# Moving splits, epilogues and scratch homes in a single-core fp32 encoder block

## The chip, the cores and the metric

One core of one Trainium2 chip runs the kernel. The metric is the device time of one execution in microseconds (us); lower is better. The engines are TensorE (PE, matmul; PEld is its weight load), VectorE (DVE), ScalarE (ACT), GpSimd (POOL) and SyncE (SP); each runs its own queue of instructions in the order in which the program issues them.

## The reference, cut to what matters

One residual block of an encoder over 256 tokens with 2048 channels, all in float32:

```python
h = x + 0.5 * swiglu(rms_norm(x, ffn1_norm), ...)      # hidden width 5632
u = rms_norm(h, mix_norm)
z_pool, q, k, v = split(u @ w_in)                      # 1024 columns each
y_pool = pool_mixer(z_pool, pool_w, pool_scale)        # 4 groups, windows 2/4/8/16
y_attn = chunk_attention(q, k, v, ...)                 # 8 heads of 128
g_pool, g_attn = split(sigmoid(u @ w_branch_gate + b_branch_gate))
h = h + (g_pool * (y_pool @ w_br_pool) + g_attn * (y_attn @ w_br_attn)) @ w_out
h = h + 0.5 * swiglu(rms_norm(h, ffn2_norm), ...)
h = h + sigmoid(rms_norm(h, ple_norm) @ w_ple_gate) * (p @ w_ple)
```

`swiglu(x, g, u, d)` is `(silu(x @ g) * (x @ u)) @ d`. Every `rms_norm` divides a token's row by its root mean square and multiplies by a gain per channel.

## The kernel before

**Matmuls in three passes.** TensorE multiplies in the float32r type, and full accuracy comes from splitting each operand into a high part (a cast) and a low part (the rest). A weight tile `wraw` of 4 x 128 rows by 512 columns is loaded by DMA; ScalarE casts it to `whi` (line 163) and VectorE subtracts to get `wlo` (line 171). `high_passes` (lines 206, 208) multiplies `whi` by the low and the high part of the activations, `low_passes` (line 213) multiplies `wlo` by the high part: twelve matmuls of 512 columns per weight tile and token tile. There are two token tiles (t = 0, 1) of 128 tokens. Two `wlo` and three `whi` buffers exist.

**Items and the stream.** An `Item` is one weight tile's work. `stream` walks a flat list and in round i issues `high` of item i+2, `low` of item i+1 and then the matmuls of item i, so the order of instructions on PE, DVE and ACT is the order written here. Loads are issued up to five items ahead, in list order, while a room for the tile is free. `seven` is an item with one token tile's worth of matmuls (twelve), `both` one with two (twenty-four).

**Blocks.** `block` computes a 1024-column output pair from the first two blocks of 512 rows with seven products instead of eight (items p1 to p7, on sums of weights made in place at lines 439, 443 and 446, called t1, t2 and t4, and on sums of activations held by `Pair`), and from the remaining rows with `both` items h[0] to h[3]. The accumulators are named a, b (second half of the columns) and e, d (first half). A feed-forward layer's hidden width is cut into parts of 4, 4 and 3 blocks of 512; in each part come the up/gate blocks and then two `down` blocks over that part. The `down` blocks of the last part of 3 have one remaining row block (`nr` = 1); all others have two. With `nr` = 2 the last item h[3] is carried over and runs as second item of the next block.

**Deferred work.** `later(n, task)` puts a task off by n steps; each `seven` takes one step and each `both` takes a step before each token tile, and a step issues the tasks that are due. If an item's operand is not there yet, it takes further steps at once (`while o.missing: step()`). `split` issues the ACT cast of an activation tile at once and its DVE subtraction one step later.

**Norms.** `Norm.turn` transposes a 128 x 512 piece of h on PE (line 506) into one of two PSUM buffers with tag `tp`, multiplies by the gain and hands the result to a `Pair` (column blocks b = 0, 1) or an `Operand` (b = 2, 3). The norms with a `home` (the first, the third and the last) build sums in `Pair.take`: for b = 1 the gained tile `gained` is, after the first norm, a `brief_tile`, which is one of the same two `tp` PSUM buffers, and so is the difference `s3` (row name `s`). `piece_tile` is a ring of five SBUF tiles.

**Mixer.** Between the projections' items the heads run as tasks: `scores`, `exps`, `shares`, `keys_down`, `values`; the four pooling groups as `means`, `read`, `group_map`. All use the two `tp` buffers.

**Launch.** `load_x` issues six dummy matmuls on the identity, loads the first norm's gain and x, turns block 0 and queues the other blocks' turns.

Of the kernel before, what the change touches and what calls it, by code (L numbers as in the profile page):

```python
# [10 lines left out]
F32 = mybir.dt.float32  # L11
# [30 lines left out]
def hybrid_block(ctx: ExitStack, tc: tile.TileContext, a: dict, out: bass.AP):  # L42
# [72 lines left out]
    def split(hi, lo, src, then):  # L115
# [119 lines left out]
    def both(banks, operand, then=None, last=False, first=False):  # L235

        def mm(it):
# [5 lines left out]
            for t, acc in enumerate(accs):  # L243
# [5 lines left out]
                low_passes(acc, forms, it.lo, last)  # L249
            if then:  # L250
                then(accs)
# [73 lines left out]
    class Pair:  # L325
# [6 lines left out]
        def __init__(self, pool, tag, home=None, other=None):  # L332
            self.pool, self.tag, self.home = pool, tag, home
# [17 lines left out]
        def take(self, half, b, t, src):  # L351
            def sums():
# [5 lines left out]
                if (b, t) == (0, 1):  # L358
                    s3 = brief_tile("s3")
# [40 lines left out]
    def block(sides, pair, rest, nr, k0, taken, done2, done1, alone=False):  # L400
# [48 lines left out]
        def rest_item(i, side, last, then=None):  # L449
# [4 lines left out]
                both(lambda: [acc(n)() for n in names], lambda: rest()[i], then, last),  # L454
            )

        end2 = lambda accs: done2(*accs)
        end1 = lambda accs: done1(*accs)
# [13 lines left out]
        if nr == 2:  # L472
            h = [rest_item(0, 1, False), rest_item(1, 1, True, end2),
                 rest_item(0, 0, False), rest_item(1, 0, True, end1)]
            return begin + [h[0], p6, p2, p7, h[1], p4, h[2]], [h[3]]
        h = [rest_item(0, 1, True), rest_item(0, 0, True)]
        p7.mm = seven(acc("b"), form("S3"),
                      lambda: (taken("u3", bank["b"]), done2(bank["e"], bank["d"])))
        p4.mm = seven(acc("b"), form("A22"), lambda: done1(bank["a"], bank["b"]), True)
        return begin + [h[0], p6, p2, p7, h[1], p4], []  # L480
# [38 lines left out]
    class Norm:  # L519
# [21 lines left out]
        def turn(self, b, t, early=False):  # L541
# [4 lines left out]
            if early or (self.home and b < 2):  # L546
                f = u.place(t) if b == 0 else (piece_tile if early else brief_tile)("gained")
# [49 lines left out]
    def load_x(norm, first_weights):  # L597
# [13 lines left out]
        for b in range(D // NB):  # L611
            norm.open(b)
            for t in token_tiles(b):
# [3 lines left out]
                else:  # L617
                    later(3 * b, task)
        for b in range(D // NB):
# [7 lines left out]
    class Parts:  # L627
# [3 lines left out]
        def __init__(self, tile_=piece_tile):  # L631
            self.tile = tile_
# [32 lines left out]
    def ffn(norm, following, gate, up, down, flat, carry, begins=False, before=None, after=None):  # L665
# [8 lines left out]
        for part, nblk in enumerate(FFN_PARTS):  # L674
# [20 lines left out]
            for j in range(nblk):  # L695
# [21 lines left out]
                else:  # L717
                    parts = Parts()

                    def done2(e, d, parts=parts):  # L720
                        parts.sg = []
                        for t, s in ((0, parts.c12(e)), (1, parts.c22(d))):
                            nc.scalar.activation(s, s, AF.Silu, scale=norm.r[t])
                            parts.sg.append(s)

                    def done1(a_, b_, j=j, parts=parts, state=state):
                        s0, s1 = parts.sg
                        h0 = parts.c11(a_)
                        nc.vector.scalar_tensor_tensor(
                            s1, b_, norm.r[1], s1, op0=ALU.mult, op1=ALU.mult  # L730
                        )
                        nc.vector.scalar_tensor_tensor(
                            h0, h0, norm.r[0], s0, op0=ALU.mult, op1=ALU.mult
                        )
                        take(j, [h0, s1], state)
# [11 lines left out]
            for n in range(0, D // NB, 2):  # L747
# [16 lines left out]
                def done2(e, d, n=n, last=last):  # L764
                    add(0, n, e)
                    add(1, n, d)
                    if last:
                        following.take(n)

                def done1(a_, b_, n=n, last=last):  # L770
                    add(0, n + 1, a_)
                    add(1, n + 1, b_)
                    if last:
# [493 lines left out]
```

## Time and profile before

| what | value |
|---|---|
| device time, median of 3 (range) | 2124.25 us (2123.97 to 2124.56) |
| device time of the profiled execution | 2124.25 us |
| its span, first to last instruction | 2122.1 us |
| PE busy | 2064.5 us, 97% of the span, 9206 matmuls |
| DVE busy | 1669.0 us, 79% |
| ACT busy | 1143.6 us, 54% |
| POOL busy | 66.0 us, 3% |
| mean granted TensorE clock | 0.991 |
| DMA | 444 MB, 209 GB/s over the span |

The busy time is the union of an engine's instructions. The device time of the profiled execution equals the median, and 2.15 us of it lie outside the span. The sites of the change are short against the whole, so stretches of a few microseconds have to be read one by one.

### The profile page before, as it was taken

The numbers are of one execution on the slowest core, as the hardware profiler recorded it, in microseconds if no ns is written. First come the engines' busy times: TensorE is split into PE (matmuls) and PEld (weight loads), VectorE is DVE, ScalarE is ACT, GpSimd is POOL, SyncE is SP. The second block draws the span as 40 slices with busy tenths as digits, with TensorE's granted clock in tenths as the row PEclk, the third lists the DMA queues.
The fourth block names the chain that finished last, engine by engine and source line by source line (L and its number), as shares of the span: only waits on it lengthen the run. The fifth ranks groups of instructions, "written<-read, shape, count | busy, mean of one in ns | idle before, by whom it ended". The sixth has DMA issues, their size and how long they took to land.

```text
span 2122.1 us, 22846 instructions
## 1 busy us (share of the span) xinstructions
PE 2064.5 (97%) x9206; PEld 1691.9 (80%) x9206; DVE 1669.0 (79%) x1259; ACT 1143.6 (54%) x988; POOL 66.0 (3%) x89
## 2 busy tenths in 40 slices
PE   7999999999999999999999999999999999999898
PEld 6888888888887788887888887888888888887677
DVE  5898888898898966554555557898888898898987
ACT  5665556555665644453434455665556655564663
POOL 0000000000000000000000000000000000000000
PEclk9999999999999999999999999999999999999999
DMA  7675677577756655554656555776577667755664
GB/s 259 217 220 196 229 257 228 179 239 253 222 180 209 217 188 192 182 169 144 204 191 198 198 183 181 258 239 215 193 264 236 198 203 265 231 193 162 224 194 159
DMA packets 222442, 444.02 MB, mean 209 GB/s; under 512 B 7480, under 2 KB 7552, under 8 KB 222336
## 3 DMA queue, kind: packets, MB, share of 16 engines
q1 hardware_dynamic: 201968, 400.59, 54.0%
q0 software_dynamic: 20368, 41.98, 10.3%
q8 instruction: 72, 1.18, 0.2%
q14 instruction: 34, 0.28, 0.0%
HBM read 440.44 MB, written 2.10 MB: 209 GB/s over the span
## 4 chain that ended last, share of the span: by engine, by line
PE 81%; DVE 13%; issue 3%; DMA 2%; ACT 1%; POOL 0%; SPq 0%; DVEq 0%; ACTq 0%; POOLq 0%
PE acc L206 8%; PE acc L208 8%; PE acc L213 8%; DVE wlo L171 7%; PE accb L206 7%; PE accb L213 7%; PE accb L208 7%; PE acce L213 5%; PE accd L206 4%; PE accd L208 4%; PE accd L213 4%; PE acca L213 4%; PE acca L206 4%; PE acca L208 4%; DVE wraw L446 4%
## 5 line engine op out<-in xcount | busy, mean ns | idle before, releaser
L171 DVE TENSOR_TENSOR wlo<-wraw,whi 128x2048 fp32r<-128x2048 f32 (+1 forms) x486 | 1099.6, 2274 | 316.3 <-PE acc L213 113.4
L163 ACT CAST whi<-wraw 128x2048 fp32r<-128x2048 f32 (+1 forms) x486 | 922.6, 1902 | 663.6 <-PE acc L208 174.7
L206 PE MATMUL acc<-whi,ulo 128*128 128x512 f32 x288 | 113.8, 395 | 0.0
L208 PE MATMUL acc<-whi,uhi 128*128 128x512 f32 x288 | 112.3, 390 | 0.0
L206 PE MATMUL acc<-whi,ual 128*128 128x512 f32 x216 | 87.5, 405 | 8.7 <-DVE ual L119 8.7
L208 PE MATMUL acc<-whi,uah 128*128 128x512 f32 x216 | 85.3, 395 | 0.0
L439 DVE TENSOR_TENSOR wraw<-wraw 128x2048 f32<-128x2048 f32 x35 | 80.2, 2292 | 1.2
L443 DVE TENSOR_TENSOR wraw<-wraw 128x2048 f32<-128x2048 f32 x35 | 80.2, 2292 | 1.2
L446 DVE TENSOR_TENSOR wraw<-wraw 128x2048 f32<-128x2048 f32 x35 | 79.9, 2283 | 0.0
L213 PE MATMUL acc<-wlo,uhi 128*128 128x512 f32 x288 | 77.1, 389 | 0.0
L206 PE MATMUL acce<-whi,ulo 128*128 128x512 f32 x184 | 73.3, 398 | 0.0
L208 PE MATMUL acce<-whi,uhi 128*128 128x512 f32 x184 | 71.8, 390 | 0.0
L206 PE MATMUL accd<-whi,ulo 128*128 128x512 f32 x184 | 71.8, 390 | 0.0
L208 PE MATMUL accd<-whi,uhi 128*128 128x512 f32 x184 | 71.7, 390 | 0.0
L206 PE MATMUL accb<-whi,ual 128*128 128x512 f32 x184 | 71.7, 390 | 0.0
L206 PE MATMUL accb<-whi,usl 128*128 128x512 f32 x184 | 71.7, 390 | 0.0
L208 PE MATMUL accb<-whi,uah 128*128 128x512 f32 x184 | 71.6, 389 | 0.0
L208 PE MATMUL accb<-whi,ush 128*128 128x512 f32 x184 | 71.6, 389 | 0.0
L206 PE MATMUL acca<-whi,ulo 128*128 128x512 f32 x184 | 71.6, 389 | 0.0
L208 PE MATMUL acca<-whi,uhi 128*128 128x512 f32 x184 | 71.6, 389 | 0.0
L206 PE MATMUL accb<-whi,ulo 128*128 128x512 f32 x184 | 71.6, 389 | 0.0
L208 PE MATMUL accb<-whi,uhi 128*128 128x512 f32 x184 | 71.6, 389 | 0.0
(332 smaller groups left out, 4211.4 us busy)
## 6 DMA issues: line engine op xcount, KB each, us to landing
wraw<-in_ffn_w_up_dram SPq DMA_DIRECT2D x88, 1024.0 KB, 7.5
wraw<-in_ffn_w_down_dram SPq DMA_DIRECT2D x88, 1024.0 KB, 9.1
wraw<-in_ffn_w_gate_dram SPq DMA_DIRECT2D x87, 1024.0 KB, 8.9
wraw<-in_w_in_dram SPq DMA_DIRECT2D x32, 1024.0 KB, 5.4
wraw<-in_w_branch_gate_dram SPq DMA_DIRECT2D x32, 1024.0 KB, 5.4
wraw<-in_ffn_w_gate_dram POOLq DMA_DIRECT2D x21, 1024.0 KB, 11.8
wraw<-in_w_out_dram SPq DMA_DIRECT2D x16, 1024.0 KB, 5.0
wraw<-in_w_ple_gate_dram SPq DMA_DIRECT2D x16, 1024.0 KB, 7.6
```

Source lines behind the costliest of these rows:

```text
L163: nc.scalar.copy(out=self.hi[:, ks, :], in_=w.raw[:, ks, :])
L171: nc.vector.tensor_tensor(out=self.lo[:, ks, :], in0=w.raw[:, ks, :], in1=self.hi[:, ks, :].bitcast(F32), op=ALU.subtract,)
L206: nc.tensor.matmul(acc, xl, wh[:, k, :], start=start and k == 0, stop=False, skip_group_check=True)
L208: nc.tensor.matmul(acc, xh, wh[:, k, :], start=False, stop=False, skip_group_check=True)
L213: nc.tensor.matmul(acc, xh, wl[:, k, :], start=False, stop=last and k == len(forms) - 1, skip_group_check=True)
L439: tt(b11.raw, b11.raw, b12.raw, op=ALU.add)
L443: tt(b11.raw, b11.raw, b22.raw, op=ALU.add)
L446: tt(b21.raw, b21.raw, b11.raw, op=ALU.add)
```

## The change

- `split` gets `at_once`: the subtraction is issued right behind the cast. The heads' `values` use it, and `group_map` of the pooling does the same for its own low part.
- `both` gets `each`, called behind each token tile's matmuls; the epilogues `done2` and `done1` of the feed-forward and the final blocks now take one token tile at a time. In the last block the outputs' order becomes t = 0, then t = 1.
- `Pair` gets `brief`: in the norms the difference `s3` is a `piece_tile` in SBUF, and so is `gained`. Hidden blocks keep the PSUM tile.
- In blocks with `nr` = 1 the order h[0], p6, p2, p7, h[1], p4 becomes p2, p6, h[0], p7, h[1], p4.
- `load_x` takes one step after block 0's turns and then issues ten dummy matmuls into the first `tp` tile.

```diff
+    def split(hi, lo, src, then, at_once=False):
         nc.scalar.copy(out=hi, in_=src)
...
-        later(1, low)
+        if at_once:
+            low()
+        else:
+            later(1, low)
...
                 low_passes(acc, forms, it.lo, last)
+                if each:
+                    each(t, acc)
...
-                    s3 = brief_tile("s3")
+                    s3 = self.brief("s3")
...
-        return begin + [h[0], p6, p2, p7, h[1], p4], []
+        return begin + [p2, p6, h[0], p7, h[1], p4], []
...
-                    self.pair = Pair(act, "u", self.home, other)
+                    self.pair = Pair(act, "u", self.home, other, piece_tile)
...
-                f = u.place(t) if b == 0 else (piece_tile if early else brief_tile)("gained")
+                f = u.place(t) if b == 0 else piece_tile("gained")
...
+            if b == 0:
+                step()
+                for _ in range(10):
+                    nc.tensor.matmul(tp[:, :P], ident, ident, start=True, stop=True)
...
-                    def done1(a_, b_, j=j, parts=parts, state=state):
-                        s0, s1 = parts.sg
-                        h0 = parts.c11(a_)
...
+                    def done1(t, acc, j=j, parts=parts, state=state):
+                        s = parts.sg[t]
+                        if t:
+                            nc.vector.scalar_tensor_tensor(
+                                s, acc, norm.r[1], s, op0=ALU.mult, op1=ALU.mult
+                            )
+                            take(j, [parts.h0, s], state)
+                        else:
+                            parts.h0 = parts.c11(acc)
+                            nc.vector.scalar_tensor_tensor(
+                                parts.h0, parts.h0, norm.r[0], s, op0=ALU.mult, op1=ALU.mult
+                            )
...
-            split(o.hi[:, hh % KB, :], o.lo[:, hh % KB, :], op[:, :SEQ], o.there)
+            split(o.hi[:, hh % KB, :], o.lo[:, hh % KB, :], op[:, :SEQ], o.there, True)
...
-                def low(yp=yp, yl=yl, yh=yh, c=c, o=o):
...
-                later(1, low)
+                nc.vector.scalar_tensor_tensor(
+                    yl, yp[:, :SEQ], col("pool_scale", c), yh.bitcast(F32),
+                    op0=ALU.mult, op1=ALU.subtract,
+                )
+                o.there()
...
+            def done1(t, acc, n=n, parts=parts, sg=sg, early=early):
+                s = late_tile("sg") if t else parts.c11(acc)
+                nc.scalar.activation(s, acc if t else s, AF.Sigmoid, scale=norm.r[t])
+                sg[1, t] = s
+                if early:
+                    embed(n + 1, t, early["accs"][t], s)
```

## Rows read from the trace of the kernel before

**Rows 1.** The page's busy times: us, share of the span, instructions.

```profile
PE 2064.5 (97%) x9206; PEld 1691.9 (80%) x9206; DVE 1669.0 (79%) x1259; ACT 1143.6 (54%) x988; POOL 66.0 (3%) x89
```

**Rows 2.** What TensorE waited for, whole span: us in total, times, longest.

```profile
PE acce L213 <- DVE wlo L171: 11.9, 15, 3.6
PE acc L206 <- DVE ual L119: 8.7, 1, 8.7
PE acce L206 <- DVE hidlo L119: 6.5, 2, 3.2
PE tp L506 <- DVE blocks L363: 5.2, 1, 5.2
PE tp L1002 <- DVE yattnlo L119: 2.7, 2, 2.0
...
PE tp L1002 <- ACT pt L948: 1.1, 1, 1.1
```

**Rows 3.** Timeline of the launch: start us, us, engine, line, operation, idle before.

```profile
6.67 1.51 DVE L549 TENSOR_TENSOR blocks<-tp,vcol 128x512 f32<-128x512 f32 x2 [0.87 <-PE tp L506]
...
8.21 0.62 ACT L116 CAST hidsh<-blocks 128x512 fp32r<-128x512 f32 x1 [0.20 <-DVE blocks L549]
8.74 1.99 ACT L163 CAST whi<-wraw 128x1024 fp32r<-128x1024 f32 x2
...
15.36 0.69 DVE L119 TENSOR_TENSOR ual<-blocks,uah 128x512 fp32r<-128x512 f32 x1
...
16.19 0.77 PE L206 MATMUL acc<-whi,ual 128*128 128x512 f32 x1 [8.74 <-DVE ual L119]
```

**Rows 4.** Busy time by stretch; PEclk is the granted TensorE clock.

```profile
16.20:24.10 7.90, 7.90 (x26) 6.35 (x27) 1.75 (x3) 1.40 (x2) 0.00 (x0) 0.70 0.82 304
...
1945.40:1952.60 7.20, 7.16 (x24) 5.75 (x25) 0.58 (x1) 0.67 (x1) 0.00 (x0) 0.76 0.00 0
...
1981.20:1992.20 11.00, 5.82 (x20) 4.85 (x21) 10.93 (x12) 8.40 (x13) 0.00 (x0) 0.69 0.27 50
```

**Rows 5.** Timeline, first block of the last part, second feed-forward.

```profile
1940.30 4.48 DVE L171 TENSOR_TENSOR wlo<-wraw,whi 128x2048 fp32r<-128x2048 f32 x2
...
1944.71 1.28 DVE L119 TENSOR_TENSOR hidlo<-tp,hidhi 128x512 fp32r<-128x512 f32 x2
...
1945.44 0.50 PE L206 MATMUL acce<-whi,hidlo 128*128 128x512 f32 x1 [3.23 <-DVE hidlo L119]
```

**Rows 6.** TensorE's timeline there: low passes of two token tiles in succession.

```profile
1966.49 1.07 PE L213 MATMUL accb<-wlo,hidhi 128*128 128x512 f32 x4
1969.21 1.07 PE L213 MATMUL accb<-wlo,hidah 128*128 128x512 f32 x4
```

**Rows 7.** Timeline, second block of that part (last norm's turns).

```profile
1982.76 2.29 DVE L171 TENSOR_TENSOR wlo<-wraw,whi 128x2048 fp32r<-128x2048 f32 x1
...
1986.38 1.09 PE L506 MATMUL tp<-ident,h 128*128 128x128 f32 x4 [5.22 <-DVE blocks L363]
...
1994.40 2.29 DVE L171 TENSOR_TENSOR wlo<-wraw,whi 128x2048 fp32r<-128x2048 f32 x1 [2.24 <-PE accd L213]
```

**Rows 8.** ScalarE's timeline there: gain multiplications into SBUF (blocks) and PSUM (gained).

```profile
1977.49 1.12 ACT L558 ACTIVATE blocks<-tp,vcol 128x128 f32<-128x128 f32 x4
...
1980.30 1.47 ACT L558 ACTIVATE gained<-tp,vcol 128x128 f32<-128x128 f32 x4
```

**Rows 9.** Timeline of the mixer, 956 to 966 us.

```profile
958.66 0.37 ACT L116 CAST yattnhi<-tp 128x256 fp32r<-128x256 f32 x1 [2.94 <-PE tp L956]
...
961.47 2.29 DVE L171 TENSOR_TENSOR wlo<-wraw,whi 128x2048 fp32r<-128x2048 f32 x1 [5.28 <-PE acc L213]
963.68 0.42 DVE L119 TENSOR_TENSOR yattnlo<-tp,yattnhi 128x256 fp32r<-128x256 f32 x1
```

**Rows 10.** Timeline of the end.

```profile
2115.84 0.69 DVE L1134 TENSOR_TENSOR sg<-acc,sg 128x512 f32<-128x512 f32 x1 [2.75 <-ACT sg L1151]
...
2117.28 1.66 SPq L1136 DMA_DIRECT2D out_dram<-h  x2
```

More of the change, by code (lines that the diff above doesn't have):

```diff
@@ L110, in step @@
             task()
-    def split(hi, lo, src, then):
+    def split(hi, lo, src, then, at_once=False):
         nc.scalar.copy(out=hi, in_=src)
@@ L233, in seven, with both @@
         return mm
-    def both(banks, operand, then=None, last=False, first=False):
+    def both(banks, operand, then=None, last=False, each=None):
         def mm(it):
@@ L325, in hybrid_block, with __init__ @@
     class Pair:
-        def __init__(self, pool, tag, home=None, other=None):
-            self.pool, self.tag, self.home = pool, tag, home
+        def __init__(self, pool, tag, home=None, other=None, brief=brief_tile):
+            self.pool, self.tag, self.home, self.brief = pool, tag, home, brief
             self.halves = [Half(self, b) for b in range(2)]
@@ L447, in t4, with rest_item @@
             b11.done()
-        def rest_item(i, side, last, then=None):
+        def rest_item(i, side, last, each=None):
             w, n0 = sides[side]
@@ L453, in rest_item, with ends @@
                 Weight(w, k0 + (2 + i) * KB, n0),
-                both(lambda: [acc(n)() for n in names], lambda: rest()[i], then, last),
+                both(lambda: [acc(n)() for n in names], lambda: rest()[i], None, last, each),
             )
-        end2 = lambda accs: done2(*accs)
-        end1 = lambda accs: done1(*accs)
+        def ends(done, names):
+            for t, n in enumerate(names):
+                done(t, bank[n])
         p1 = Item(b11, seven(acc("b"), form("A11"), tell("p1", "b")), [b11, b12], [t1], keep=True)
@@ L631, in __init__ @@
         def __init__(self, tile_=piece_tile):
-            self.tile = tile_
+            self.tile, self.sg = tile_, {}
         def taken(self, name, acc):
@@ L718, in ffn, with done2 @@
                     parts = Parts()
[L720 to L724, printed above, removed]
-                    def done1(a_, b_, j=j, parts=parts, state=state):
-                        s0, s1 = parts.sg
-                        h0 = parts.c11(a_)
[L729 to L735, printed above, removed]
+                    def done2(t, acc, parts=parts):
+                        s = (parts.c22 if t else parts.c12)(acc)
+                        nc.scalar.activation(s, s, AF.Silu, scale=norm.r[t])
+                        parts.sg[t] = s
+                    def done1(t, acc, j=j, parts=parts, state=state):
[10 more added lines that the diff above has]
+                            )
                     main, left = block(
@@ L762, in taken, with done2, done1 @@
                         add(1, n, acc, -0.5)
[L764 to L767, printed above, removed]
+                def done2(t, acc, n=n, last=last):
+                    add(t, n, acc)
+                    if last and t:
                         following.take(n)
[L770 to L773, printed above, removed]
+                def done1(t, acc, n=n, last=last):
+                    add(t, n + 1, acc)
+                    if last and t:
                         following.take(n + 1)
```

30 lines of the change are left out of this document (8 added, 22 removed).

## The prediction

> **What bounds the kernel now.** I read the page first: TensorE is busy 97% of the span [rows 1], so the most that any reordering can give back is TensorE's idle time, about 58 us, the end included. Then the waits of TensorE over the whole span [rows 2], to see who ends that idle time. The reader is to see that it isn't spread evenly. One group is a comb of waits for VectorE's `wlo` (11.9 us in 15), which the diff leaves alone in the blocks with `nr` = 2. The others are single holes: 8.7 us at the launch, twice 3.2 for `hidlo`, 5.2 for a `tp` buffer, a few in the mixer. Last I read the timeline around each hole, with the granted clock of the stretches, to see what the late instruction stands behind in its queue.
>
> One token tile's twelve matmuls take 2.72 us at the full clock: two successive low passes start at 1966.49 and 1969.21 [rows 6]. Call this a pass; a `seven` is one, a `both` two.
>
> **The change part by part.**
>
> *Launch.* The first product needs `ual`, which is issued one step after the cast, so behind both weight tiles' subtractions: it runs at 15.36, although `whi` started at 8.74 [rows 3]. TensorE idles 8.7 us, and then has the lower clock: in 16.2 to 24.1 the granted clock is 0.70 of full [rows 4], so 0.30 x 7.9 = 2.4 us are lost.
> With the added step VectorE does `ual`, `hidsl` and the difference s3 (0.6 to 0.7 us each) straight after its two gain multiplications, which end at 8.18: until 10.1. The cast of s3 (0.6) now stands in ScalarE's queue ahead of `whi`, whose first half comes at 11.7 instead of 9.7. The first product starts near 11.8: 4.4 us earlier. The ten dummies are fp32 of 128 columns; they follow the turns, whose eight matmuls end at 7.45. At the half clock a pair takes 0.5 us, as the first six took (12 instructions in about 2.9 us), at the full clock half of it, so the dummies end between 10.1 and 12.4. That is before or just after the product could start: they cost 0 to 0.6 and keep TensorE active in the hole. If the clock is full then, the whole 2.4 comes back less about 0.5 for the later `wlo`, and the gain is 6.3. If the engine falls to 1.2 GHz anyway for a few microseconds, it is 3.2 to 4.9. I take 5.8; bounds 3.2 to 6.6.
>
> *Blocks with `nr` = 1, first of each layer.* h[0] reads the third hidden block, whose transposes are issued two and three steps after the carried item. In the old order h[0] comes at once behind p3, takes further steps to get its operand, and its low parts stand behind two `wlo` (4.48 us from 1940.30) [rows 5]. With p2 and p6 ahead, the two low parts have two passes, 5.4 us, to be made in, and the hole was 3.2: it goes, in both layers. What moves with it: p2's load of `b21` goes ahead of h[0]'s in SP's list; its room is freed by the previous p4, some eight items earlier, and nothing waits behind it longer than now. t2, which p6 reads, has one item more ahead of it (p2) and lies two items back. p7 now follows a `both`, so t4 (2.29) is covered by two passes and the wait of 0.1 at h[1] goes too: 3.3 us per layer. In the second layer the clock after the hole was 0.76 over 7.2 us [rows 4], 1.7 us lost: 5.0 there. Bounds from zero clock effect to 1 us of small delays more: 3.2 to 4.4, and 3.4 to 6.0.
>
> *Second of these blocks, last norm.* TensorE waits 5.22 us for a `tp` buffer [rows 7]: `gained` sits in it until VectorE has subtracted and differenced it. In SBUF it holds no PSUM buffer, and this wait goes. But what is late next is VectorE: it is busy 10.93 of the 11.0 us around the hole [rows 4]. Before, five `wlo` had to be done for p1, p3, p5, h[0] and p6, which are six passes; in the new order p1, p3, p5, p2 and p6 need the same five `wlo` and are five passes. So for the same products TensorE needs one `wlo` (2.29) more from a VectorE that has no room. The gain is at most 5.2 - 2.3 = 2.9, or 2.2 if read as the 2.24 us that VectorE itself waited just after [rows 7] and now fills; at the low end new waits at p2 and p6 eat it all. I take 2.5; bounds 0 to 5.2. In the first layer the mixer's norm has no home, so its second block only gains the 0.1 at h[1] and a little order: 0.4, bounds -0.5 to 0.9.
> The four `gained` tiles also change their writer's target. Four pieces into PSUM take 1.47 us on ScalarE, into SBUF 1.12 [rows 8]: 0.35 less each, off the path where ScalarE has room, so nothing is counted.
> The Trainium skill, page "ScalarE: Activation LUTs", section "Step-by-step: what each stage is for", says the opposite: a ScalarE write to PSUM is faster than one to SBUF. By it these tiles would get dearer on ScalarE; by the row they get cheaper by 0.35. The trace does not agree with it for a group of four, and the sum is the same by either, since ScalarE has idle time around them.
>
> *Mixer.* The heads' low part leaves a `tp` buffer occupied until a step later, behind a `wlo`: the cast is done at 959.0, the subtraction runs at 963.68 behind the `wlo` from 961.47 [rows 9], and the pooling map waits 2.0 us for it; another 0.7 and, for the buffer of `pt`, 1.1 are of the same kind some 20 us before [rows 2]. At once, the subtraction runs near 959.1 and both buffers are free when the map comes: 2.7 + 1.1 = 3.8. VectorE now waits for ScalarE's cast in its queue; behind it stand the `wlo`, which themselves waited 5.28 us for a buffer [rows 9], so the wait is covered. Without that cover it would be the cast, 0.4, for each of 8 heads: 3 us. The pooling's low parts keep their place behind the same `wlo`, so the two waits around 985 us (a `tp` buffer, a DMA of pooling weights, 3.0 together) stay. 3.8; bounds 1.0 to 4.5.
>
> *Epilogues by token tile.* In the 31 blocks with `nr` = 2 the first tile's epilogue now stands ahead of the next step's tasks. At h[1] no task stands there, at h[3] VectorE may do its first two operations (0.7 each) during the second pass. No hole of [rows 2] lies behind them, so nothing, bounds -2 to 1.
>
> *End.* Of the last two output tiles the t = 1 one is now last and alone: its multiplication starts at 2115.84 and its DMA is issued at 2117.28 as now; the second tile's two operations and DMA, which end the old program (the pair of DMA issues lasts 1.66) [rows 10], go in front. 1.66 less one issue of 0.33: 1.3; bounds 0.8 to 1.5.
>
> **Sum.** 5.8 + 3.3 + 0.4 + 3.8 + 5.0 + 2.5 + 1.3 = 22.1 us. The profiled execution took 2124.25, equal to the median, so 2124.25 - 22.1 = 2102.2.
>
> **The rivals.**
> *VectorE takes over in the reordered blocks.* For it: 10.93 of 11.0 us [rows 4]. Against: it idles 2.24 us right after [rows 7]. Then the second blocks give nothing, and p2 or p6 waits also in the first ones: 2.5 + 0.4 + about 3 less, 2108.
> *The launch gains little.* s3's cast holds back `whi`, and the clock falls anyway, in the gap between dummies and product. For it: 8.7 us without matmuls is what it fell after. Against: the gap becomes 2 us at most. 3.2 or less instead of 5.8: 2105 to 2108.
> *It does not do what it should:* b21's load, moved ahead, is late, and p2 waits in the hole's place. A load takes some 5 to 9 us to land; the room comes free about 20 us before p2. If it does decide, 3.3 + 5.0 + 2.9 are lost: 2113.
> *Slower:* the early epilogue blocks VectorE. It is in order, so an epilogue that waits for the first pass holds the step's tasks, and behind them the next `wlo`, on which the comb of waits hangs. There are 62 such epilogues. At 0.36 us each it eats 22.1 and decides; at 0.5 the time is 2133. Against: before, two epilogues after the second pass stood ahead of the same `wlo`, and few tasks fall on those steps.
>
> **How the numbers follow.** The forecast with all five gains: 0.60. VectorE in the reordered blocks 0.14, little at the launch 0.14, the load 0.05, slower or nothing from the epilogues 0.07. The time is that of the first: 2102.2. All upper bounds together give about 2124.3 - 29, but not all meet: 2095 at the low end. At the high end the second and third cases give 2108, and lower bounds of two terms 2110. A difference under 0.2%, 4.25 us, can't be told from no change; faster means below 2120.0: all of the first four cases, 0.93. Within 0.2%: 0.04, slower 0.03, both from the epilogues' rival.
>
> **What would show it.** In the changed profile the first real product should start near 12 us, and the granted clock stay above 0.9 until 24. The waits for `hidlo`, `blocks` and `yattnlo` should be gone from TensorE's list, and the waits of p2 and p6 for `wlo` in the last part be new, some 1 to 2.5 us each. The wait of 3.6 for `wlo` at the last norm's reciprocal root stays, and so do those of the pooling weights. The last output DMA should be one, 1.3 us after the other's old place at most. I am wrong if VectorE's busy share rises without TensorE's, if `wlo` waits more than double, or if the blocks with `nr` = 2 get longer.

## The result

The changed kernel takes 2100.76 us (median of 4 runs, 2100.06 to 2101.72) beside 2124.4 us (4 runs, 2123.97 to 2126.38) for the kernel before: the ratio is 0.9887, 95% interval 0.987 to 0.9904. Its profiled execution took 2100.06 us with a span of 2098.0, so 24.1 us went out of the span.

The page's busy times of the changed kernel answer to [rows 1]. TensorE is 4.3 us less busy (it has twenty instructions more, and ran fewer stretches at the lower clock); VectorE has the same work in a shorter span.

```profile
PE 2060.2 (98%) x9226; PEld 1691.0 (81%) x9226; DVE 1669.5 (80%) x1259; ACT 1142.5 (54%) x988; POOL 66.0 (3%) x89
```

What TensorE waits for in the changed kernel, whole span, as in [rows 2]:

```profile
PE acce L216 <- DVE wlo L174: 12.2, 16, 3.6
PE accb L216 <- DVE wlo L174: 3.1, 2, 2.3
...
PE tp L1013 <- DMA gw<-in_pool_w_dram: 2.0, 1, 2.0
PE acca L216 <- DVE wlo L174: 2.0, 2, 1.6
...
PE acc L209 <- DVE ual L119: 1.1, 1, 1.1
PE tp L999 <- DVE ypoollo L1022: 1.1, 1, 1.1
PE acc L209 <- ACT whi L166: 0.8, 1, 0.8
...
PE tp L1013 <- ACT pt L959: 0.3, 1, 0.3
```

The big single holes of [rows 2] are gone: 8.7 us for `ual`, twice 3.2 for `hidlo`, 5.2 for `blocks`, 2.7 for `yattnlo`. New are 3.1 us of waits for `wlo` in the accumulator b, 1.1 for `ual` and 0.8 for `whi`; those for `wlo` in a have grown from 0.8 to 2.0. The comb on acce is as it was.

To see where the time went, I cut the span at the starts of matmuls that both traces have: the third weight tile's first, then p3 and the following p1 of each pair of `nr` = 1 blocks, the mixer's first projection and so on. The stretches are the differences of those starts, in us. "First" and "second" are the two `nr` = 1 blocks; the mixer's stretch is its heads and pooling; "end" runs from the last matmul's start.

| kernel | launch | first (ffn1) | second (ffn1) | mixer | first (ffn2) | second (ffn2) | last stage | end |
|---|---|---|---|---|---|---|---|---|
| before | 30.79 | 30.13 | 37.98 | 67.90 | 31.71 | 42.20 | 102.02 | 7.45 |
| changed | 26.03 | 25.94 | 36.72 | 63.89 | 25.94 | 39.81 | 101.60 | 6.11 |
| order only | 30.76 | 25.94 | 37.19 | 69.17 | 25.94 | 39.91 | 101.24 | 7.45 |
| homes only | 30.28 | 31.73 | 38.01 | 66.33 | 31.55 | 40.62 | 101.23 | 7.44 |
| no dummies | 26.23 | 25.94 | 37.17 | 65.50 | 25.94 | 39.87 | 101.84 | 6.09 |
| no step | 30.81 | 25.94 | 37.19 | 65.26 | 25.94 | 39.85 | 101.46 | 5.99 |
| old order in the second blocks | 26.15 | 25.94 | 37.82 | 65.07 | 25.94 | 40.89 | 101.39 | 6.02 |
| heads' split late | 26.12 | 25.94 | 37.15 | 68.36 | 25.94 | 39.82 | 101.80 | 5.98 |
| pooling's split late | 26.06 | 25.94 | 36.72 | 63.97 | 25.94 | 39.81 | 101.49 | 6.12 |
| epilogues behind both tiles | 26.11 | 25.94 | 37.16 | 65.02 | 25.94 | 39.87 | 101.46 | 5.99 |
| less VectorE | 26.04 | 25.94 | 34.40 | 62.21 | 25.94 | 37.65 | 99.06 | 6.03 |
| old order at the end | 26.00 | 25.94 | 36.67 | 62.21 | 25.94 | 39.81 | 102.35 | 7.45 |

The stretches left out (the rest of both feed-forwards and the projections) are the same to 0.3 us in all of these. The gains of the changed kernel are so 4.76 at the launch, 4.19 and 1.26 in ffn1, 4.01 in the mixer, 5.77 and 2.39 in ffn2, 0.42 in the last stage and 1.34 at the end, which is the whole 24.1 us. Two of them are in part the clock's: in ffn1's second block five other kernels with the same order have 37.15 to 37.19 us at a granted clock of 0.95, where the changed kernel has 1.00, so 0.8 of the 1.26 us are the change's; and the last stage takes 101.23 to 102.35 us in all the kernels but the one with less VectorE, whichever epilogues they have. The table also shows how far one execution's total can be trusted. Among kernels whose mixer waits alike, that stretch takes 62.2, 63.9 or 65.0 to 65.5 us: the granted clock over it is 1.00 at 62.21, 0.97 at 63.89 and 0.95 at 65.07. Totals differ by 3 us for that alone, so below an edit is judged by its own stretch. Where the clock is alike the mixer's gain is nearly the same: 66.33 against 62.21 us at 1.00, 67.90 against 63.89 at 0.97, and 69.17 against 65.0 to 65.5 at 0.95.

The launch of the changed kernel, as in [rows 3]:

```profile
7.65 3.75 PE L630 MATMUL tp<-ident 128*128 128x128 f32 x20
...
10.60 0.62 ACT L116 CAST ush<-s 128x512 fp32r<-128x512 f32 x1 [1.36 <-DVE s L365]
11.12 5.61 ACT L166 CAST whi<-wraw 128x1024 fp32r<-128x1024 f32 x4
...
12.21 0.50 PE L209 MATMUL acc<-whi,ual 128*128 128x512 f32 x1 [0.81 <-ACT whi L166]
...
14.58 0.38 SPq L147 DMA_DIRECT2D wraw<-in_ffn_w_up_dram  x1
...
20.89 1.91 ACT L166 CAST whi<-wraw 128x2048 fp32r<-128x2048 f32 x1 [4.16 <-DMA wraw<-in_ffn_w_up_dram]
...
26.03 0.50 PE L209 MATMUL acc<-whi,ual 128*128 128x512 f32 x1 [1.13 <-DVE ual L119]
```

The first product starts 3.98 us earlier, behind the s3 cast (`ush`) and the first half of `whi`. Eleven microseconds on, a part is given back: ScalarE stands 4.16 us at the cast of a weight tile whose transfer was issued at 14.58, the casts of the next activations wait behind it, and the third tile waits 1.13 us for `ual`.

Busy times by stretch, as in [rows 4]: the launch's first 7.9 us of products, the 11 us around the old hole of the second block, and the whole second block of ffn2.

```profile
12.20:20.10 7.90, 7.89 (x38) 6.35 (x39) 7.14 (x5) 4.53 (x3) 0.00 (x0) 1.00 1.05 386
...
1962.50:1973.50 11.00, 7.08 (x23) 5.30 (x23) 10.97 (x12) 9.88 (x12) 0.00 (x0) 0.84 0.00 0
1950.43:1990.25 39.82, 34.77 (x152) 27.11 (x150) 38.28 (x32) 27.13 (x40) 1.28 (x1) 0.96 0.59 188
```

The reader is to see the clock at 1.00 instead of 0.70 at the launch, and VectorE busy 38.28 of the second block's 39.82 us. The DMA share of 1.05 instead of 0.82 is no gain, since the stretch lies 4 us earlier: the kernel before has 1.05 (387 GB/s) from 12.2 to 20.1 too.

### The profile page after: what moved, and what is told of

It reads as the page before. It is cut to its first block, busy times and chain, and to the rows that moved or that the text cites. A ratio compares the mean times of both kernels' runs of the same rounds, so it can differ in the third digit from the quotient of the medians.

```text
span 2098.0 us, 22891 instructions
## 1 busy us (share of the span) xinstructions
PE 2060.2 (98%) x9226; PEld 1691.0 (81%) x9226; DVE 1669.5 (80%) x1259; ACT 1142.5 (54%) x988; POOL 66.0 (3%) x89
## 4 chain that ended last, share of the span: by engine, by line
PE 82%; DVE 13%; issue 3%; ACT 1%; DMA 0%; POOL 0%; DVEq 0%; POOLq 0%; ACTq 0%
PE acc L209 9%; PE acc L211 9%; PE acc L216 8%; DVE wlo L174 7%; PE accb L216 7%; PE accb L211 7%; PE accb L209 7%; PE acce L216 4%; PE acca L211 4%; PE accd L211 4%; PE acca L209 4%; PE accd L209 4%; PE acca L216 4%; PE accd L216 4%; DVE wraw L451 3%
```

## The experiments

### The order alone, and the homes alone

The kernel before with one edit each; first the order, then `gained` and s3 in SBUF.

```diff
-        return begin + [h[0], p6, p2, p7, h[1], p4], []
+        return begin + [p2, p6, h[0], p7, h[1], p4], []
```

> The kernel before with the new order in the blocks with nr = 1 and nothing else. My theory: the holes for hidlo go in both layers, worth 4.2 and 5.8 us as the changed kernel's trace shows; in the second of these blocks the wait of 5.2 us for a tp buffer stays, because gained and s3 are still in PSUM, and it now stands before p2, so the last-norm block gains less than 0.5; the mixer-norm block gains about 1. Sum 10 to 11.5, so 2113 to 2114.5 us. Rival: the order itself gives the last-norm block's 2.4 us too; then 2111 and no wait for tp over 3 us.

```diff
-                    s3 = brief_tile("s3")
+                    s3 = self.brief("s3")
...
-                f = u.place(t) if b == 0 else (piece_tile if early else brief_tile)("gained")
+                f = u.place(t) if b == 0 else piece_tile("gained")
```

> The kernel before with gained and s3 of the norms in SBUF and nothing else. Theory of the prediction (VectorE is the bound behind the tp wait): the 5.2 us wait goes, TensorE waits instead for wlo at h[0] by 1 to 2 us, and p6, p2 behind the two passes of h[0] don't wait; gain 2 to 4, so 2120.3 to 2122.3. Rival (the tp buffer alone was the cause): all 5.2 and the lower clock behind it come back, 6 to 7 us, 2117.5.

Measured: 2111.84 and 2121.31 us beside 2123.77. The first blocks gain 4.19 and 5.77 us by the order; with the homes alone ffn1's is 1.6 longer (its granted clock is 0.95 there, beside 1.00 before) and ffn2's 0.16 shorter. That part is the order's alone. In the second block of ffn2 each edit alone gives most of what both give: 2.29 and 1.58, both together 2.39. TensorE's waits in that block, first of the order-only kernel, then of the homes-only one:

```profile
PE tp L506 <- DVE blocks L363: 5.2, 1, 5.2
PE tp L506 <- DVE h L750: 0.7, 1, 0.7
```

```profile
PE accd L206 <- DVE h L750: 1.9, 1, 1.9
PE acce L213 <- DVE wlo L171: 1.8, 2, 1.6
PE tp L506 <- DVE h L750: 0.8, 1, 0.8
PE acca L213 <- DVE wlo L171: 0.7, 1, 0.7
```

With the order alone the 5.2 us wait for the `tp` buffer stands as before, and still 2.29 us of 2.39 are there; with the homes alone it is gone and four other waits for VectorE make 5.2 us, much as that run's theory had it. So the theory that the order gives next to nothing there while that wait stands fell; the rival had the block's gain, but not that the wait would stay. The wait that the prediction took away is not what the block's length hangs on.

### VectorE's work in the second blocks

The changed kernel with the old order put back in the second blocks only:

```diff
-        return begin + [p2, p6, h[0], p7, h[1], p4], []
+        first = [h[0], p6, p2] if alone else [p2, p6, h[0]]
+        return begin + first + [p7, h[1], p4], []
```

> The changed kernel with the order of before (h0, p6, p2) put back in the two second nr=1 blocks only; the first nr=1 blocks keep the new order. Theory (VectorE's amount of work sets the length of the second blocks, and with the homes changed the order no longer matters there): the second block of ffn2 stays within 0.4 us of the changed kernel's 32.3 us from its first product to its h[1], its TensorE waits stay near 5.0 us in sum and only change their places, and the time stays within 0.5 us of 2100.8. Rival (order and homes each bring a part there, as the 1.6 us of the homes alone beside the 2.4 us of both suggests): 0.8 us come back in the second block of ffn2 and up to 1.2 us in that of ffn1, so that the time is 2101.5 to 2102.8. The first blocks gain 4.2 and 5.8 us in both.

And the changed kernel without one add of t1 in the blocks that nothing is carried into:

```diff
-            tt(b11.raw, b11.raw, b12.raw, op=ALU.add)
+            if not alone:
+                tt(b11.raw, b11.raw, b12.raw, op=ALU.add)
```

> The changed kernel with the add of b12 to b11 (one VectorE instruction of 2.29 us on 128x2048) left out in the blocks that nothing is carried into: the two second nr=1 blocks and the first block behind the mixer's and the last feed-forward's end. Their p5, p6, p7 and p4 so use other weights than the reference's. Theory (VectorE is busy 38.3 of the 39.8 us of ffn2's second block, and its amount of work sets that block's length): TensorE's waits in that block fall from 5.0 to 2.6 to 3.0 us, the block's 39.8 us become 37.4 to 37.9, ffn1's second block loses its 0.8 us wait, and the time is 2096 to 2098. Rival (a late weight tile or transposed operand sets the waits, and VectorE is only the messenger): the waits in ffn2's second block stay within 0.5 us of 5.0, and the time is 2100 to 2101.

Measured: 2103.16 and 2090.92 us. Without the one VectorE instruction of 2.29 us the second blocks are 2.32 and 2.16 us shorter and the last stage 2.54. Its waits in the second block of ffn2, after those of the changed kernel there:

```profile
PE accb L216 <- DVE wlo L174: 2.3, 1, 2.3
PE acca L216 <- DVE wlo L174: 2.0, 2, 1.6
PE tp L514 <- ACT sq L589: 0.7, 1, 0.7
```

```profile
PE accb L216 <- DVE wlo L174: 2.3, 1, 2.3
PE acca L216 <- DVE wlo L174: 0.7, 2, 0.4
```

The sum goes from 5.0 to 3.0. The theory's stretch came out as written (37.4 to 37.9 expected, 37.65 measured). The add's removal also lets the next weights' cast start earlier, but VectorE's own idle time in the block is 1.56 us beside 1.54: the block shrank by VectorE's work. And the block of the changed order takes 39.81 us in the kernel with the old order at the end, whose granted clock there is 1.00, and 39.81 to 39.87 at 0.96. So VectorE's amount of work sets this block. The same edit left the add out of two blocks more, the kernel's first and the one behind the mixer. VectorE is busy for 31.8 and 32.7 of 40 us around them, and nothing was gained: the left-out stretches that hold them take 629.84 and 940.47 us, beside 629.91 and 940.40 in the changed kernel. The total fell below the expected 2096 to 2098 because I had priced ffn1's second block at 0.8 us only, left the last stage's first block, which has the add too, out of the sum, and the mixer ran at the full clock.

With the old order in the second blocks 1.10 and 1.08 us come back, much as the rival had it, at waits of TensorE that sum to the same (4.9 beside 5.0 us in ffn2), as the theory had it. In ffn1 some 0.45 of the 1.10 us are the clock's (0.95 beside 1.00), and the total holds 1.2 us of the mixer's besides. In ffn2 the granted clock is 0.92 beside 0.96:

```profile
1952.72:1993.61 40.89, 35.85 (x151) 27.85 (x150) 38.37 (x32) 26.57 (x39) 1.28 (x1) 0.92 0.54 170
```

But the order-only kernel has 0.91 in its block and takes 39.91 us, so the clock by itself doesn't explain this last microsecond. VectorE's row does: it is idle for 2.52 us of this block, beside 1.54 in the changed kernel and 1.57 in the order-only one. What it waits for in the block of the old order:

```profile
DVE wlo L174 <- PE accd L216: 1.6, 1, 1.6
DVE wlo L174 <- PE accb L216: 0.8, 1, 0.8
```

These `wlo` wait for TensorE to finish with their buffer. In the new order VectorE has no such wait in this block, only two of 0.7 us for ScalarE. So the order's part is that VectorE, which sets the block's length, stands still for a microsecond less.

### The launch: dummies and step

The changed kernel without the ten dummies, and without the added step:

```diff
-                for _ in range(10):
-                    nc.tensor.matmul(tp[:, :P], ident, ident, start=True, stop=True)
```

> The changed kernel without its ten new dummy matmuls; the added step stays. My theory: the first product still starts near 12.2 us, but TensorE is idle for over 4 us before it, the granted clock falls, and the first 24 matmuls run partly at 1.2 GHz: 1.5 to 2.5 us lost at the start of the second weight tile, 2102.5 to 2103.5. Rival: the eight turns at the launch hold the clock, or VectorE's subtraction bounds the first tile anyway; then no loss over 0.5 us.

```diff
             if b == 0:
-                step()
                 for _ in range(10):
```

> The changed kernel without the added step at the launch; the ten dummies stay. My theory: the low parts of block 0 stand behind both weight tiles' subtractions again, the first product starts at 15 to 16.2 us as before, and the dummies can't bridge that, so the clock falls too: 4 to 6 us lost, 2105 to 2107. Rival: the dummies are what mattered, the clock stays full over the hole, and only the start is late, with part of it caught up by the first blocks' slack: 2 us or less.

Measured: 2102.73 and 2106.44 us. The rows below are the first product and the third tile's first matmul without the dummies, then the first product without the step.

```profile
11.59 0.79 PE L209 MATMUL acc<-whi,ual 128*128 128x512 f32 x1 [4.36 <-ACT whi L166]
...
26.23 0.50 PE L209 MATMUL acc<-whi,ual 128*128 128x512 f32 x1
```

```profile
16.56 0.76 PE L209 MATMUL acc<-whi,ual 128*128 128x512 f32 x1 [5.91 <-DVE ual L119]
```

Without the dummies the product starts at 11.59, which is within the 11.35 to 12.50 of the kernels that have them. Its matmuls take 0.79 and 0.63 us until 16.5, where those behind the dummies take 0.50 and 0.40; by their length that is the lower clock, though the row of the granted clock reads 1.00 there. The third tile starts 0.20 us later, and that is all that the dummies are worth: the rival was right. The total of 2102.73 lies in the theory's range all the same, because the mixer took 65.50 us in this execution. Without the step the launch takes 30.81 us, as the theory had it: its whole gain but those 0.20 us is the step's. In the six other kernels with this launch the third tile starts between 26.00 and 26.15, although the first product starts anywhere from 11.35 to 12.50. What holds it there is the transfer that ScalarE waits for.

### The mixer: heads and pooling

The changed kernel with the heads' low part deferred again, and with the pooling's low parts deferred again:

```diff
-            split(o.hi[:, hh % KB, :], o.lo[:, hh % KB, :], op[:, :SEQ], o.there, True)
+            split(o.hi[:, hh % KB, :], o.lo[:, hh % KB, :], op[:, :SEQ], o.there)
```

> The changed kernel with the low part of the attention output's split deferred by a step again, all else kept. Theory (the at-once split frees the two op buffers, and this alone gave the mixer's gain): the waits for yattnlo and pt of the kernel before (2.7 and 1.1 us) stand again between 930 and 955 us, 3.8 to 4.1 us come back, and the time is 2104.6 to 2104.9. Rival (the waits come from the order of the pooling's turns beside the heads, and the deferral costs little by itself): under 1.5 us come back, and the time is at most 2102.3.

```diff
-                nc.vector.scalar_tensor_tensor(...)
-                o.there()
+                def low(yp=yp, yl=yl, yh=yh, c=c, o=o):
+                    nc.vector.scalar_tensor_tensor(...)
+                    o.there()
+
+                later(1, low)
```

> The changed kernel with the low parts of the pooling's split deferred by a step again. Theory (the mixer's gain is that of the attention's split alone): the stretch from 920 to 985 us changes by less than 0.5 us. Rival (both splits are needed, as the last pooling group is waited for by the branch's product): 1.5 us or more come back there, the more so where a step holds a whole product.

Measured: 2105.06 and 2100.09 us. With the heads late the mixer takes 68.36 us, 4.47 more than in the changed kernel and 0.46 more than before (the granted clock is 0.98, 0.97 and 0.97). Of TensorE's waits in it, these two have grown or are new:

```profile
PE tp L1013 <- DVE ypool L1022: 3.1, 2, 2.0
...
PE tp L1013 <- ACT pt L959: 1.1, 1, 1.1
```

They are the 2.7 and 1.1 us of [rows 2], the first under another releaser's name and 0.4 longer. The head's low part still holds one of the two `tp` buffers, so the pooling's next map needs the other one, and that is freed by the pooling's own low part, which now stands ahead of the head's and behind the `wlo`:

```profile
952.11 2.29 DVE L174 TENSOR_TENSOR wlo<-wraw,whi 128x2048 fp32r<-128x2048 f32 x1 [5.29 <-PE acc L216]
954.32 0.48 DVE L1022 SCALAR_TENSOR_TENSOR ypool<-tp,vcol,ypool 128x256 fp32r<-128x256 f32 x1
...
954.85 1.13 PE L1013 MATMUL tp<-df,gw 128*128 128x256 f32 x4 [1.98 <-DVE ypool L1022]
...
956.93 0.41 DVE L119 TENSOR_TENSOR yattnlo<-tp,yattnhi 128x256 fp32r<-128x256 f32 x1
```

The pooling's low parts alone make no difference (63.97 beside 63.89). The mixer's gain is the heads' split.

### Epilogues and the end

The changed kernel with the epilogues of `both` after both token tiles, and with the last stage's epilogue in the order of before:

```diff
-                if each:
+            if each:
+                for t, acc in enumerate(accs):
                     each(t, acc)
```

> The changed kernel with the epilogues of both token tiles after both tiles' products again, all else kept. Theory (the early epilogues are worth the end of the kernel and nothing else): the time from the last matmul to the last output DMA's issue is 1.3 us longer, every other stretch is the same to 0.2 us, and the time is 2102.0 to 2102.2. Rival (the early epilogues stand in VectorE's queue where it is the bound, and cost there): the second nr=1 blocks are 0.7 us or more shorter without them, and the time is 2100.0 to 2101.4.

```diff
             def done1(t, acc, n=n, parts=parts, sg=sg, early=early):
-                s = late_tile("sg") if t else parts.c11(acc)
-                nc.scalar.activation(s, acc if t else s, AF.Sigmoid, scale=norm.r[t])
-                sg[1, t] = s
-                if early:
-                    embed(n + 1, t, early["accs"][t], s)
+                if not t:
+                    sg["a"] = acc
+                    return
+                for t, acc in ((1, acc), (0, sg["a"])):
+                    s = late_tile("sg") if t else parts.c11(acc)
+                    nc.scalar.activation(s, acc if t else s, AF.Sigmoid, scale=norm.r[t])
+                    sg[1, t] = s
+                for t in (1, 0):
+                    if early:
+                        embed(n + 1, t, early["accs"][t], sg[1, t])
```

> The changed kernel, in which the last stage's epilogue of the second side takes its instructions in the order of before: tile 1's sigmoid, tile 0's add and sigmoid, then the embedding products of tile 1 and of tile 0. Theory (the end's gain is the order in the queues of ScalarE and VectorE, since tile 0's product is done 2 us before tile 1's): the stretch from the last matmul's start to the end of the span goes from 6.1 us back to 7.3 to 7.5. Rival (the end gains from something else, such as a shorter wait of the output's transfers): it stays at 6.0 to 6.2. The rest of the kernel is untouched in both.

Measured: 2101.38 and 2100.39 us. The first total is what the rival allowed, and both theory and rival were wrong: the end stays at 5.99 us, the second blocks are no shorter, and what the total has more than the changed kernel's profiled execution lies in the mixer (65.02 beside 63.89) and in ffn1's second block (37.16 beside 36.72), both at a clock of 0.95. An engine's queue holds only the order of its own instructions; where they stand in the program among PE's matters only for the tasks that they so pass. With the old order the end goes back to 7.45, as expected. The end of the changed kernel, then of the one with the old order at the end:

```profile
2090.28 0.72 ACT L1159 ACTIVATE p<-p,nr 128x512 f32<-128x512 f32 x1 [6.97 <-DVE p L663]
...
2092.27 0.69 ACT L1159 ACTIVATE sg<-accb,nr 128x512 f32<-128x512 f32 x1 [1.27 <-PE accb L216]
2092.48 2.29 SPq L1144 DMA_DIRECT2D out_dram<-h  x2
```

```profile
2091.26 0.69 ACT L1163 ACTIVATE sg<-accb,nr 128x512 f32<-128x512 f32 x1 [9.08 <-PE accb L216]
2091.84 0.71 ACT L1163 ACTIVATE p<-p,nr 128x512 f32<-128x512 f32 x1
...
2093.42 1.66 SPq L1144 DMA_DIRECT2D out_dram<-h  x2
```

In the changed kernel tile 0's sigmoid runs while tile 1's last matmuls do; in the old order it stands behind tile 1's in ScalarE's queue, though its input was ready 2 us before.

### Two versions that were to be faster

On top of the changed kernel: the second up tile goes into the empty room `wa`, the dummies into an accumulator bank, the launch's s3 split comes a step later, and the norm's root two steps later.

```diff
+                    ups[1].weight.tag = "wa"
...
-                    nc.tensor.matmul(tp[:, :P], ident, ident, start=True, stop=True)
+                    nc.tensor.matmul(spare[:, :P], ident, ident, start=True, stop=True)
...
-                    self.sum(2, s3)
+                    if self.launch:
+                        later(1, lambda: self.sum(2, s3))
+                    else:
+                        self.sum(2, s3)
...
-                            following.done()
+                            later(2, following.done)
```

> A new version on top of the changed kernel: the second up tile of the first product is loaded into the still empty room wa (its transfer was issued when a room came free), the dummies write an accumulator bank instead of the bank of the first transposes, the S3 operand of the launch is split a step later, and the norm's root after each feed-forward is put two steps later, behind the next weights' low parts in VectorE's queue. Theory (the 1.13 us wait at the third tile is the late load's, the 0.78 us one the held bank's, and the 3.55 us wait at the last norm is VectorE's queue standing at the root that waits for ScalarE): 1.1 to 2.2 us at the launch and 2.4 to 3.1 us at the last norm, 2095.5 to 2097.5. Rival (the last stage's first block has to wait for its weights or transposes all the same, and the transfers at the launch are bound by their rate, not their issue): under 1.5 us in all, 2099.3 or more.

On top of that, t1's add by an accumulating transfer in the second blocks:

```diff
-            tt(b11.raw, b11.raw, b12.raw, op=ALU.add)
+            if alone and nr == 1:
+                nc.gpsimd.dma_start(b11.raw, b12.src, accum_op=ALU.add)
+            else:
+                tt(b11.raw, b11.raw, b12.raw, op=ALU.add)
...
+        if alone:
+            return [p1, p3, p2, p5, p6, h[0], p7, h[1], p4], []
```

> The version above, and in the two second nr=1 blocks the add of b12 to b11 is made by an accumulating transfer from DRAM instead of VectorE, with p2 between p3 and p5 to give it time. Theory (VectorE's amount of work sets these blocks): each is 1.8 to 2.3 us shorter, as without that add, and the time is 3.5 to 4.6 us under the version above. Rival (the transfer lands too late: ScalarE's queue stands at the cast of p5's weights, and what is behind it is late): 0 to 1 us under it, or above it.

Measured: 2103.65 us (4 runs, 2103.32 to 2103.82; ratio to before 0.9895, interval 0.9878 to 0.9911), and 2126.39 us (10 runs, 2123.95 to 2128.15; ratio 1.0, interval 0.999 to 1.0009). Both totals are what the rivals had. Against the changed kernel the first version is longer by 0.92 us at the launch, 1.23 between ffn1's second block and the mixer, and 1.68 in the last stage. Timeline of the first version at the launch and behind the last norm:

```profile
18.48 1.34 PE L517 MATMUL tp<-ident,h 128*128 128x128 f32 x8 [3.19 <-DMA h<-in_x_dram]
...
2003.49 0.15 DVE L604 TENSOR_REDUCE ssum<-ssq 128x2 f32<-128x8 f32 x1
...
2005.71 1.12 DVE L579 SCALAR_TENSOR_TENSOR ulo<-tp,vcol,uhi 128x128 fp32r<-128x128 f32 x4
...
2006.88 1.11 PE L517 MATMUL tp<-ident,h 128*128 128x128 f32 x4 [4.32 <-DVE ulo L579]
```

The weight tile came earlier, and TensorE then waited 3.2 us for the next pieces of x, which the turns need; from 20.1 to 24.0 its granted clock was 0.69, and the third tile started at 26.95 instead of 26.03. The second version has the same launch, and there the third tile started at 25.16:

```profile
18.31 1.07 PE L522 MATMUL tp<-ident,h 128*128 128x128 f32 x8 [1.62 <-DMA h<-in_x_dram]
```

Its first product came at 10.96 instead of 9.17, the wait was 1.6 us and the clock stayed at 1.00. So one and the same launch gained 0.9 us or lost 0.9, mostly by the clock behind the wait, and the theory's 1.1 to 2.2 us came in neither. In both the turns start at 18.3 to 18.5 with the DMA engines busy all the while (share 1.05, 386 to 389 GB/s from 10 to 20 us), which is what the rival's bound by the rate would look like; no run sets the rate apart. The move of the root costs in both norms. At the last one the root, moved from in front of the weights' low parts, now stands in front of the norm's own low parts (`ulo`), which free the `tp` buffer of the next turns: 3.6 us of wait became 0.3 there and 4.3 here. The mixer's norm has a new wait of 1.0 us for `ulo`. Of the second version, the accumulating transfer's issue and the cast that reads its result:

```profile
1961.46 1.28 POOL L448 DMA_DIRECT2D wraw<-in_ffn_w_down_dram  x1 [1.28 <-DVE wlo L174]
...
1979.64 1.90 ACT L166 CAST whi<-wraw 128x2048 fp32r<-128x2048 f32 x1 [12.54 <-DMA wraw<-in_ffn_w_down_dram]
```

Eighteen microseconds lie between them, where 2.29 us of VectorE stood, and ScalarE's queue stands with them; TensorE waits 22.0 us for such casts in the two blocks. The second blocks take 47.87 and 52.26 us, so this version says nothing on what an add less on VectorE is worth.

## Why the prediction was right, point by point

*Launch.* The term of 5.8 us was mis-sized; it measured 4.76, inside its bounds. First product near 11.8 (12.21; 11.35 to 12.50 in the other kernels with this launch) and the full clock from there (1.00) came as told. What I left out is the next limit: once the first two tiles run early, the third waits for the transfer of the second up tile, which left SP's queue at 14.58. The 2.4 us of clock, which the dummies were to bring back, are for the most part waited away there: without the dummies 0.20 us are lost, not 2.4. The rival "the launch gains little" saw s3's cast ahead of `whi`, which is there as a wait of 0.8 us, but its conclusion didn't follow.

*First blocks.* 4.19 and 5.77 us for the 3.3 and 5.0 that I took. All kernels with the order, whatever else they have, come to 25.94 us in either layer. The hole was rightly read, but I priced only the hole and, in ffn2, the clock behind it. In ffn1 the granted clock was 1.00 over the block before too; there TensorE's idle time of 3.46 us went, and its busy time fell from 26.67 to 25.94 for the same matmuls. Probably this is the restart: the matmul behind the hole takes 0.50 us instead of 0.39, and the one ahead of a hole runs out alone. No run tests it apart.

```profile
655.94:681.88 25.94, 25.94 (x123) 21.45 (x122) 23.64 (x17) 14.43 (x17) 0.00 (x0) 1.00 0.41 148
```

TensorE has no idle time left in that stretch of the changed kernel. The rival of a late `b21` has no wait to show.

*Second blocks.* 2.39 us for 2.5 in ffn2, 1.26 for 0.4 in ffn1, of which 0.8 are not the clock's. "What is late next is VectorE" was right and stronger than I had it, but that the number in ffn2 is so near is partly luck. I subtracted a `wlo` from the removed 5.2 us wait. The runs show that the 5.2 us wait needn't be removed at all: with it in place, the order gives 2.29. The order, which I took to cost a `wlo`, gives nearly all of the gain alone, and in its kernel VectorE's waits of 2.2 and 0.8 us for TensorE are gone from this block. VectorE is busy nearly throughout, so whichever wait is taken away comes back under another name until the block is as long as VectorE's work, and one instruction less there is worth its full 2.2 to 2.3 us. The new waits came at 1.6 and 2.3 us, in accumulators a and b, as the prediction asked for p2 and p6.

*Mixer.* 4.01 for 3.8, by the heads' split, as told; the pooling's part is worth nothing and its waits of 2.0 and 1.1 us stayed, as told. The 0.2 more lies within what the clock does there: at like clocks the gain is 4.1, 4.0 and 3.7 to 4.2.

*Homes and ScalarE.* The group of four goes faster into SBUF, as the row of before had it:

```profile
1959.31 1.16 ACT L566 ACTIVATE gained<-tp,vcol 128x128 f32<-128x128 f32 x4
```

That is 1.16 us instead of the 1.47 into PSUM [rows 8]. But the single instruction is the shorter one into PSUM. In the kernel before, 1960 to 2000 us, with busy time and mean ns of one behind the bar, `gained` goes to PSUM and `blocks` to SBUF; the third line is `gained` of the changed kernel, 1940 to 1980 us, into SBUF:

```profile
L558 ACT ACTIVATE gained<-tp,vcol 128x128 f32<-128x128 f32 x8 | 2.7, 341 | 0.2
L558 ACT ACTIVATE blocks<-tp,vcol 128x128 f32<-128x128 f32 x8 | 2.2, 359 | 0.0
...
L566 ACT ACTIVATE gained<-tp,vcol 128x128 f32<-128x128 f32 x8 | 2.3, 380 | 0.0
```

Eight of 341 ns fill 2.7 us, so they run one behind the other; eight of 359 or 380 fill 2.2 or 2.3, so they overlap. The rule of the Trainium skill that the prediction weighed ("ScalarE: Activation LUTs", section "Step-by-step: what each stage is for") calls PSUM the port of lower latency. The trace agrees for one instruction and not for the time of the group, which the prediction counted. No wait of TensorE in either kernel's list is put down to these tiles on ScalarE.

*Epilogues and end.* Nothing in the blocks, and 1.34 at the end for the 1.3 that I took. The mechanism was the order of the two tiles in ScalarE's and VectorE's queues, as the prediction worked it out; issuing each tile's epilogue between the passes does nothing by itself. The rival on the slower side has nothing to show: the stretches with the 31 blocks of two remaining row blocks are the same to 0.3 us.

The sum was 22.1, and 24.1 came in the profiled executions (23.6 between the medians): 1.0 too much at the launch, and 1.7, 0.9, 0.2 and 0.4 too little in the first blocks, the second of ffn1, the mixer and the last stage, where the clock is 0.98 beside 0.97. That the sum is within 2 us is in part luck: an error of 1.0 in one direction meets 3.2 in the other, and some 0.9 us of the 3.2, in ffn1's second block and the last stage, are what the clock did in this execution.

## What to carry to other kernels

When an engine is busy for the whole of a stretch, price a change there by the work it takes off that engine and not by the wait that it removes: the wait returns under another name, and two edits that each remove it don't add up. Behind a hole at the launch look for the next transfer, since clock and start time gained ahead of it may only be waited away. Read the time of a group of instructions and that of one apart: here the target with the shorter instruction had the longer group. Judge an experiment by its own stretch; here a total agreed with a rival's while its stretch showed something else.

## What was unexpected of the hardware

Kernels with the same waits behind the mixer's heads ran that stretch in 62.2, 63.9 or 65.0 to 65.5 us, at a granted clock of 1.00, 0.97 and 0.95; it is the largest part of the difference between the totals of kernels that do the same there. An accumulating transfer of 1 MB took 18.2 us from issue to the cast that reads it in a stretch where plain loads landed in 13.5 (median of three issued there); there the accumulating ones, of which two were under way, landed in 15.7 (median), and in the changed kernel the single one issued around the same block in 9.9. Without the dummies at the launch matmuls ran at half the pace from 11.6 to 16.5 us while the row of the granted clock read 1.00: the length of the matmuls has to be read beside that row.
